# A two-layer token-mixing trunk on one core: hand-set issue order ahead of attention, convolution and pooling sums behind it

## Chip, cores and metric

The kernel runs on one NeuronCore of a Trainium2 chip, in one launch. The metric is the device time of an execution in microseconds (us). The names of the engines in the profile are PE (TensorE, matmuls; PEld its weight loads), DVE (VectorE), ACT (ScalarE), POOL (GpSimd) and SP (SyncE, which here only issues loads and stores).

## What is computed

A trunk of two layers on 512 tokens of 1024 channels, in float32. Each layer mixes the tokens in three branches that are merged by gates, and then runs a wide feed-forward block:

```python
def layer(x, l):
    h = rms_norm(x, g_mix[l])
    proj = h @ w_in[l]
    u_pool, q_lat, kv_lat, u_lru, gate_logit = split(proj)      # 256, 384, 256 + 32, 256, 3 * 1024 columns
    y_pool = pool_mixer(u_pool) @ w_pool_proj[l]                 # means over the last 2, 4, 8, 16 tokens, minus u
    y_mla = attention(q_lat, kv_lat) @ w_mla_o[l]                # 8 heads, causal, rotary part of 32 columns
    y_lru = rg_lru(u_lru) @ w_lru_proj[l]                        # convolution over 4 tokens, gates, linear recurrence
    gates = sigmoid(gate_logit + b_gate[l])                      # three times 1024 channels
    x = x + (gates[0] * y_pool + gates[1] * y_mla + gates[2] * y_lru) @ w_out[l]
    h = rms_norm(x, g_ffn[l])
    return x + square(relu(h @ w_ff1[l])) @ w_ff2[l]             # 4096 inner channels
```

A final norm follows the second layer.

## The kernel before

Channels lie on the 128 partitions, the 512 tokens along the free axis, so x is eight blocks of 128x512. To keep float32's precision, every operand of a matmul is split into a high and a low part in the matmul's reduced format: ScalarE casts the high part, and VectorE (in places POOL) subtracts it from the source. A product is then three matmuls: high by high, high by low, low by high (`three`, `dense`). The split blocks of x, times the norm's gain, are xhm and xlm.

Weights come from DRAM in chunks of 128x1024, one load each on SP's queue into a ring of three buffers (`raw`); `chunk` splits each into whi and wlo, two buffers each (N_W). A chunk thus can be split only when the matmuls of the chunk two before it have been read out.

In the order of the program a layer has these stages:

1. `mixer`, ahead of attention: in_0 to in_9 are the projections of the input (the compressed keys and values ckv, the rotary key kr, the compressed queries ql, the LRU's input, the pooling's input). The norm's factor, rstd, is applied to their results, so they need not wait for it; it is found from the sum of squares of x (`sumsq`: squares on ScalarE, added on POOL), whose sum over partitions is the matmul totm. totckv and totql are the same for the two latent norms. `lru_in` takes in_6 and in_7 through the convolution into u (one scaling and three multiply-adds on VectorE each); `pool_in` takes in_8 and in_9 through the sums over windows on POOL into pm.
2. Attention, head by head: va are the values, ka and qn, qr make keys and queries, s are the scores in four blocks of queries, p the probabilities (minimum and sum on VectorE, exponential on ScalarE), t their transposes, split into pt0h and pt0l (one pair for all heads), o the output. Head h ends with ob, the sum of o's two halves, split into ot (high part on ScalarE, low part on POOL, line 155 by way of line 458). Ahead of heads 0, 2, 4 and 6 stands a gate in the program.
3. `merge`: 24 gates ga_jb in all (24 matmuls each, a product with rstd on VectorE, a tanh on ScalarE), and, once nine of them are issued (LRU_N), `pool_lru_out`: the LRU's two gates for each of two halves (ra_00 to ra_11, three matmuls each), its recurrence, and the pooling's small product (pa). Then `project` combines the branches (pj) and the output projection follows (wo).
4. The feed-forward block (f).

The text is not issued in that order: a scheduler, which simulates the program, orders each engine's instructions when the program is built, within what the data, the buffers and the pools of memory allow. Engines then run their instructions strictly in that order. A pool of memory that is opened later (`mg`, merge) may take the room of one that is closed (`at`, attention); its first writer waits for the last user of that room. The matmuls accumulate in PSUM: three buffers `acc`, two each for scores and transposes, one for o.

The lines that the change touches most:

```python
            a0, a1 = project(C_CKV, "s"), project(C_CKV + 1, "s")
            norm_x(f"m{l}", rstd, sumsq_x(f"m{l}"))
            if l == 0:
                setup_late()
                setup_vectors()
...
            lru_in(0)
            qlat = latent_norm(zq, V_GQ, QR, "ql")
            lru_in(1)
            pool_in(0)
            pool_in(1)
```

`setup_vectors` makes the LRU's constants from its parameters, in some twenty operations of 128x4 on VectorE.

Of the kernel before, what the change touches and what calls it, by code (L numbers as in the profile page):

```python
# [15 lines left out]
P = 128  # L16
D = 1024
# [27 lines left out]
# order of the weight chunks of a layer, each [128, 1024] with the contraction on partitions  # L45
# [7 lines left out]
# columns of the per-channel vectors of a layer  # L53
# [5 lines left out]
# columns of the constants  # L59
# [5 lines left out]
def trunk(ctx: ExitStack, tc, x_in, wts, vecs, consts, out):  # L65
# [12 lines left out]
    # ---- constants and per-channel vectors  # L78
# [15 lines left out]
    # blocks of x and gates share their buffers: x waits in DRAM while the branches are computed  # L94
# [11 lines left out]
    # ---- helpers  # L106
# [37 lines left out]
    def dense(dst, w, acts, off=0):  # L144
        """dst[m, t] = sum_k w[k, m] * act[k, t]"""
        terms = []
        for k, (h, lo_) in enumerate(acts):
            terms += three(blk(w[0], off + k), blk(w[1], off + k), h, lo_)
        matmuls(dst, terms)

    def split(src, hi, lo, scale=None, eng=nc.vector):
        """hi + lo = src * scale, each float32r"""
        if scale is None:
            nc.scalar.copy(hi, src)
            eng.tensor_tensor(lo, src, f(hi), op=ALU.subtract)
        else:
            nc.scalar.activation(hi, src, AF.Copy, scale=scale)
            nc.vector.scalar_tensor_tensor(lo, src, scale, f(hi), op0=ALU.mult, op1=ALU.subtract)  # L158

    def sumsq(blocks, name):  # L160
        s = tmpp.tile([P, S], F32, tag="ssq", bufs=2, name=f"ssq{name}")
        for i, b in enumerate(blocks):
            if i == 0:
                nc.scalar.activation(s, b, AF.Square)
            else:
                q = tmp(f"sq{name}{i}")
                nc.scalar.activation(q, b, AF.Square)
                nc.gpsimd.tensor_tensor(s, s, q, op=ALU.add)
        return s

    def rsqrt_mean(s, n, dst, name):
# [3 lines left out]
        tot = acc(f"tot{name}", "o", 1)  # L175
        matmuls(tot, [(ones, h), (ones, lo)])
        rsqrt(tot, n, dst, name)
# [9 lines left out]
    def sumsq_x(name):  # L187
        return sumsq(x, name)
# [7 lines left out]
    def gained(l, col, name):  # L196
        res = []
        for k in range(KB):
            h = xsp.tile([P, S], F32R, tag="xh", bufs=KB, name=f"xh{name}{k}")
# [5 lines left out]
    def setup():  # L205
        nc.scalar.dma_start(vec, vecs)
        nc.vector.memset(epst, EPS)
        nc.scalar.copy(warm, epst)
        nc.vector.memset(f(ones), 1.0)
        # the first two chunks come by halves, between the first blocks of x  # L210
        raws = [wpool.tile([P, 1024], F32, tag="raw", bufs=N_RAW, name=f"raw0_{c}") for c in range(2)]
        for k in range(KB):
            nc.sync.dma_start(x[k], x_in[k])
            if k < 4:
                c, cols = k // 2, slice(512 * (k % 2), 512 * (k % 2) + 512)
                nc.sync.dma_start(raws[c][:, cols], wts[0, c, :, cols])
        for c in range(2):
            hi, lo = ready[0, c] = wtiles(0, c)
            for i in range(2):
                cols = slice(512 * i, 512 * i + 512)  # L220
                nc.scalar.copy(hi[:, cols], raws[c][:, cols])
                nc.vector.tensor_tensor(lo[:, cols], raws[c][:, cols], f(hi[:, cols]), op=ALU.subtract)
        nc.sync.dma_start(cst, consts)
# [545 lines left out]
```

## Time and profile before

| | |
|---|---|
| median of 3 runs | 1408.4 us |
| runs | 1408.29, 1408.40, 1409.72 us |
| profiled execution, first to last instruction (span) | 1406.1 us |
| TensorE busy | 1379.1 us (98%) |
| VectorE busy | 773.8 us (55%) |
| ScalarE busy | 559.7 us (40%) |
| POOL busy | 320.7 us (23%) |
| mean granted TensorE clock | 0.998 |

The span is that of one execution, taken by the profiler; the time of a run is measured around the whole execution, and for the profiled one only the span is shown. The median run is 2.3 us longer than that span. Busy times overlap, since the engines run side by side; the share of TensorE is an average over stages, and what a change in one stage is worth has to be read from that stage. Matmul records are longer (0.39 us for 512 columns) than the distance from one to the next, because they are pipelined.

### The profile page before, as it was taken

The numbers are of one execution on the slowest core, as the hardware profiler recorded it, in microseconds if no ns is written. First come the engines' busy times: TensorE is split into PE (matmuls) and PEld (weight loads), VectorE is DVE, ScalarE is ACT, GpSimd is POOL, SyncE is SP. The second block draws the span as 40 slices with busy tenths as digits, with TensorE's granted clock in tenths as the row PEclk, the third lists the DMA queues.
The fourth block names the chain that finished last, engine by engine and source line by source line (L and its number), as shares of the span: only waits on it lengthen the run. The fifth ranks groups of instructions, "written<-read, shape, count | busy, mean of one in ns | idle before, by whom it ended". The sixth has DMA issues, their size and how long they took to land.

```text
span 1406.1 us, 16117 instructions
## 1 busy us (share of the span) xinstructions
PE 1379.1 (98%) x6252; PEld 1142.1 (81%) x6252; DVE 773.8 (55%) x1122; ACT 559.7 (40%) x847; POOL 320.7 (23%) x234
## 2 busy tenths in 40 slices
PE   7999999999999999999999999999999999999997
PEld 5877888888888888888887878888888888888886
DVE  8978774574544234443368887655745433344323
ACT  5457683324332112323244777632333221232322
POOL 3265101132322002211115530111232200022112
PEclk9999999999999999999999999999999999999999
DMA  5321122253332323233332212223423233333231
GB/s 200 100 79 61 57 79 100 91 155 100 94 102 92 104 90 105 90 112 113 121 104 85 72 58 73 90 90 105 150 90 105 91 104 90 105 90 105 91 103 62
DMA packets 42124, 137.38 MB, mean 98 GB/s; under 512 B 4672, under 2 KB 6848, under 8 KB 42048
## 3 DMA queue, kind: packets, MB, share of 16 engines
q1 hardware_dynamic: 41328, 135.76, 30.6%
q8 instruction: 49, 0.80, 0.2%
q10 hardware_dynamic: 720, 0.59, 0.1%
q14 instruction: 27, 0.22, 0.0%
HBM read 132.14 MB, written 4.19 MB: 97 GB/s over the span
## 4 chain that ended last, share of the span: by engine, by line
PE 91%; DVE 6%; issue 1%; ACT 1%; DMA 0%; DVEq 0%; ACTq 0%
PE f L116 50%; PE ga L116 17%; PE wo L116 6%; PE pj L116 6%; PE in L116 5%; PE s L116 2%; PE o L452 1%; DVE wlo L138 1%; PE t L444 1%; DVE q L420 1%; PE qr L116 1%; PE ka L116 1%; PE qn L116 1%; DVE qll L158 1%; DVE p L438 0%
## 5 line engine op out<-in xcount | busy, mean ns | idle before, releaser
L137 ACT CAST whi<-raw 128x1024 fp32r<-128x1024 f32 (+1 forms) x236 | 246.7, 1045 | 687.4 <-issue 381.9
L138 DVE TENSOR_TENSOR wlo<-raw,whi 128x1024 fp32r<-128x1024 f32 (+1 forms) x236 | 307.0, 1301 | 162.3 <-ACT whi L137 162.2
L116 PE MATMUL f<-al,whi 128*128 128x512 f32 (+1 forms) x528 | 202.2, 383 | 0.0
L116 PE MATMUL f<-ah,whi 128*128 128x512 f32 (+1 forms) x528 | 202.0, 383 | 0.0
L116 PE MATMUL f<-ah,wlo 128*128 128x512 f32 (+1 forms) x528 | 202.0, 383 | 0.0
L116 PE MATMUL f<-xhf,whi 128*128 128x512 f32 x512 | 199.2, 389 | 0.0
L116 PE MATMUL f<-xlf,whi 128*128 128x512 f32 x512 | 199.2, 389 | 0.0
L116 PE MATMUL f<-xhf,wlo 128*128 128x512 f32 x512 | 199.2, 389 | 0.0
L622 POOL TENSOR_TENSOR ft<-ft 128x512 f32<-128x512 f32 x64 | 94.4, 1477 | 426.9 <-ACT ah L621 426.9
L116 PE MATMUL ga<-xhm,whi 128*128 128x512 f32 x384 | 151.3, 394 | 2.5 <-ACT q L415 2.5
L116 PE MATMUL ga<-xhm,wlo 128*128 128x512 f32 x384 | 151.2, 394 | 0.0
L116 PE MATMUL ga<-xlm,whi 128*128 128x512 f32 x384 | 150.6, 392 | 0.0
L116 PEld LDWEIGHTS f<-al,whi 128*128 128x128 f32 x528 | 99.2, 188 | 19.5
L116 PEld LDWEIGHTS f<-ah,wlo 128*128 128x128 f32 x528 | 99.2, 188 | 19.4
L116 PEld LDWEIGHTS f<-ah,whi 128*128 128x128 f32 x528 | 99.2, 188 | 19.2
L116 PEld LDWEIGHTS f<-xlf,whi 128*128 128x128 f32 x512 | 96.1, 188 | 20.0
L116 PEld LDWEIGHTS f<-xhf,wlo 128*128 128x128 f32 x512 | 96.1, 188 | 20.0
L116 PEld LDWEIGHTS f<-xhf,whi 128*128 128x128 f32 x512 | 96.1, 188 | 19.9
L618 DVE SCALAR_TENSOR_TENSOR ft<-f,rstdf 128x512 f32<-128x512 f32 x64 | 44.1, 692 | 102.1 <-PE f L116 102.0
L116 PEld LDWEIGHTS ga<-xhm,whi 128*128 128x128 f32 x384 | 72.2, 188 | 17.6 <-ACT q L415 3.0
L116 PEld LDWEIGHTS ga<-xlm,whi 128*128 128x128 f32 x384 | 72.2, 188 | 14.3
L116 PEld LDWEIGHTS ga<-xhm,wlo 128*128 128x128 f32 x384 | 72.2, 188 | 14.3
(366 smaller groups left out, 2119.8 us busy)
## 6 DMA issues: line engine op xcount, KB each, us to landing
raw<-wts SPq DMA_DIRECT2D x232, 512.0 KB, 3.5
x<-x_in SPq DMA_DIRECT2D x8, 256.0 KB, 5.4
xr<-x_in SPq DMA_DIRECT2D x8, 256.0 KB, 2.9
saved<-xr SPq DMA_DIRECT2D x8, 256.0 KB, 2.0
xr<-saved SPq DMA_DIRECT2D x8, 256.0 KB, 3.1
out<-xr SPq DMA_DIRECT2D x12, 128.0 KB, 1.8
raw<-wts SPq DMA_DIRECT2D x4, 320.0 KB, 2.9
raw<-wts SPq DMA_DIRECT2D x4, 256.0 KB, 4.5
```

The source lines that it names most:

```text
L116: ins = nc.tensor.matmul(dst, lhsT=a, rhs=b, start=(start and i == 0), stop=(stop and i == n - 1))
L137: nc.scalar.copy(hi[:, :cols], raw[:, :cols])
L138: nc.vector.tensor_tensor(lo[:, :cols], raw[:, :cols], f(hi[:, :cols]), op=ALU.subtract)
L158: nc.vector.scalar_tensor_tensor(lo, src, scale, f(hi), op0=ALU.mult, op1=ALU.subtract)
L420: eng.tensor_tensor(q[o:o + ROPE], qr[src], table[src], op=ALU.mult)
L444: nc.tensor.transpose(tp[:, j, :], blk(probs[i], j), ident)
L452: nc.tensor.matmul(o[:, q0 * P:], lhsT=v[j][:, h, :, :], rhs=pt[c][:, 3 * j + q0:3 * j + 4, :], start=(j == 0 and c == 0), stop=(j == 3 an ...
L618: nc.vector.scalar_tensor_tensor(t, a, 0.0, rstd, op0=ALU.max, op1=ALU.mult)
L622: nc.gpsimd.tensor_tensor(t, t, t, op=ALU.mult)
```

## The change

It has four parts.

**The start.** TensorE gets ten matmuls on a constant block (N_BUSY) ahead of everything else, into the buffers of the transposes. The halves of the first two chunks are loaded in another order among the blocks of x, and the constants come behind the third chunk. in_0 and in_1 go by blocks of x, in turn. `setup_vectors` moves to the merge, behind the first gate that is issued there.

**Ahead of attention.** In a `manual_schedule` PE, DVE and ACT issue in the order of the text. In layer 0 VectorE adds the squares of x, in both layers those of the latents. The sums totm, totckv and totql stand in the middle of in_3, in_5 and in_7, chunks are split one step ahead (`prefetch`), and kr's weights are split in two halves outside the chunks' buffers. in_6 and in_7 are only scaled into u_0 and u_1, in_8 and in_9 into pm_0 and pm_1.

**Behind attention.** The convolution (`conv`, into new tiles cu in the merge's pool) and the sums over windows (`windows`, in place into pm) stand at the head of the merge.

**The branches' small products.** `pool_lru_out` becomes `lru_out` (at nine gates) and `pool_out` (at eleven, POOL_N), each with its own part of the small chunk, so that chunk comes in two loads.

```diff
+N_BUSY = 10
 LRU_N = 9
+POOL_N = 11
+ORDERED = {mybir.EngineType.PE, mybir.EngineType.DVE, mybir.EngineType.Activation}
...
     def setup():
+        busy = tmp("busy", F32R)
+        nc.vector.memset(f(busy), 1.0)
+        nc.vector.memset(epst, EPS)
+        for i in range(N_BUSY):
+            matmuls(acc(f"busy{i}", "t", 2), [(blk(busy, 0), busy)])
...
+        parts = [(c, slice(512 * i, 512 * i + 512)) for i in range(2) for c in range(2)]
         for k in range(KB):
             nc.sync.dma_start(x[k], x_in[k])
-            if k < 4:
-                c, cols = k // 2, slice(512 * (k % 2), 512 * (k % 2) + 512)
-                nc.sync.dma_start(raws[c][:, cols], wts[0, c, :, cols])
+            if k in (0, 3):
+                for c, cols in parts[:2] if k == 0 else parts[2:]:
+                    nc.sync.dma_start(raws[c][:, cols], wts[0, c, :, cols])
...
+            with tc.manual_schedule(engines=ORDERED):
+                if l == 0:
+                    a0, a1 = (acc(f"in{l}_{C_CKV + i}", "s") for i in range(2))
+                    w = [chunk(l, C_CKV + i) for i in range(2)]
+                    for k in range(KB):
+                        for a, c in zip((a0, a1), w):
+                            matmuls(a, three(blk(c[0], k), blk(c[1], k), *xs[k]), start=k == 0, stop=k == KB - 1)
...
+                if l == 0:
+                    ssq = sumsq_x(f"m{l}", nc.vector)
+                prefetch(C_QL)
+                kra = acc(f"in{l}_{C_KR}")
+                matmuls(kra, [(wkr[k], v) for k in range(KB) for v in xs[k]])
+                tot = total(ssq, f"m{l}")
+                prefetch(C_QL + 1)
+                q0, tot = project(C_QL, mid=tot)
...
+                scaled(project(C_LRU), us[0])
+                prefetch(C_POOL)
+                a, tot = project(C_LRU + 1, mid=tot)
...
+                for b in range(2):
+                    pm.append(tmpp.tile([P, S], F32, tag="ssq", bufs=2, name=f"pm{l}_{b}"))
+                    scaled(project(C_POOL + b), pm[b])
...
+    def conv(l, late, us):
+        res = []
+        for b, z in enumerate(us):
+            u = late.tile([P, S], F32, name=f"cu{l}_{b}")
+            cw = lambda j: vcol(l, V_CW + 2 * j + b)
+            nc.vector.tensor_scalar(u, z, cw(3), vcol(l, V_CB + b), op0=ALU.mult, op1=ALU.add)
+            for j in (2, 1, 0):
+                o = 3 - j
+                nc.vector.scalar_tensor_tensor(u[:, o:], z[:, :S - o], cw(j), u[:, o:], op0=ALU.mult, op1=ALU.add)
+            res.append(u)
+        return res
+
+    def windows(l, late, pm):
...
+        for b, z in enumerate(pm):
+            cur = padded(f"pz{l}_{b}", slice(0, P))
+            nc.scalar.copy(cur[:, 8:], z)
...
+            nc.gpsimd.tensor_tensor(z, win, z, op=ALU.subtract)
...
         res = []
         gates = list(early)
+        us = conv(l, mg, us)
+        windows(l, mg, pm)
         for n in range(3 * KB):
             if n == LRU_N:
-                py, ly = pool_lru_out(l, mix, us, pm)
+                ly = lru_out(l, mix, us)
+            if n == POOL_N:
+                py = pool_out(l, mix, pm)
             if n >= len(early):
                 gates.append(gate(l, rstd, xs, n))
+            if l == 0 and n == len(early):
+                with tc.issue_after(last_gate[0]):
+                    setup_vectors()
```

Three places show what becomes of the order. The first is PE in layer 0 at the last head's output, o_7 (from the split probabilities pt0h, pt0l and the values v); ga_41 is a gate's sum, ra are the LRU's gates from the split convolution lyh, lyl. Before:

```order
L452 MATMUL o_7_1628<-pt0h,v_0_689 128x512
L116 MATMUL ga_41_2034<-xhm_136,whi_33_2037 128x512
L116 MATMUL ga_41_2034<-xlm_137,whi_33_2037 128x512
L116 MATMUL ga_41_2034<-xhm_136,wlo_33_2038 128x512
L452 MATMUL o_7_1628<-pt0l,v_0_689 128x512
L452 MATMUL o_7_1628<-pt0h,v_1_699 128x384
L452 MATMUL o_7_1628<-pt0l,v_1_699 128x384
L452 MATMUL o_7_1628<-pt0h,v_2_709 128x256
L452 MATMUL o_7_1628<-pt0l,v_2_709 128x256
L452 MATMUL o_7_1628<-pt0h,v_3_719 128x256
L452 MATMUL o_7_1628<-pt0l,v_3_719 128x256
L116 MATMUL ga_41_2034<-xhm_140,whi_33_2037 128x512
```

With the change:

```order
L505 MATMUL o_7_1588<-pt0h,v_3_679 128x256
L505 MATMUL o_7_1588<-pt0l,v_3_679 128x256
L119 MATMUL ra_00_1859<-lyh_0_1853,whi_15_1849 128x512
L119 MATMUL ra_01_1864<-lyh_0_1853,whi_15_1849 128x512
L119 MATMUL ra_10_1887<-lyh_1_1881,whi_15_1849 128x512
L119 MATMUL ra_00_1859<-lyl_0_1854,whi_15_1849 128x512
L119 MATMUL ra_00_1859<-lyh_0_1853,wlo_15_1850 128x512
L119 MATMUL ra_01_1864<-lyl_0_1854,whi_15_1849 128x512
L119 MATMUL ra_01_1864<-lyh_0_1853,wlo_15_1850 128x512
L119 MATMUL ra_10_1887<-lyl_1_1882,whi_15_1849 128x512
L119 MATMUL ra_10_1887<-lyh_1_1881,wlo_15_1850 128x512
L119 MATMUL ra_11_1892<-lyh_1_1881,whi_15_1849 128x512
```

Where a gate's matmuls stood between and behind those of o_7, the LRU's twelve now follow them directly; behind the last (three of ra_11) come the 24 of ga_30, the 24 of ga_31, the six of pa, and ga_32.

The second is DVE where the convolution is made (L337 and L340 before, L520 and L523 now). Before, between the scaling of in_6 and in_7 and the norm of the queries:

```order
L277 TENSOR_TENSOR lz_0_470<-in_6_472,rstdm_156 128x512
L138 TENSOR_TENSOR wlo_8_590<-raw_8_587,whi_8_589 128x1024
L337 TENSOR_SCALAR u_0_168<-lz_0_470,vec 128x512
L340 SCALAR_TENSOR_TENSOR u_0_168<-lz_0_470,vec,u_0_168 128x512 x3
L277 TENSOR_TENSOR lz_1_546<-in_7_548,rstdm_156 128x512
L337 TENSOR_SCALAR u_1_169<-lz_1_546,vec 128x512
L138 TENSOR_TENSOR wlo_9_633<-raw_9_630,whi_9_632 128x1024
L340 SCALAR_TENSOR_TENSOR u_1_169<-lz_1_546,vec,u_1_169 128x512
L183 SCALAR_TENSOR_TENSOR ntql_525<-totql_521,ntql_525 128x512
L340 SCALAR_TENSOR_TENSOR u_1_169<-lz_1_546,vec,u_1_169 128x512
L184 TENSOR_SCALAR ntql_525<-ntql_525 128x512
```

With the change, behind the sum of head 7's output:

```order
L510 TENSOR_TENSOR ob_7_1597<-ob_7_1597,o_7_1588 64x512
L520 TENSOR_SCALAR cu_0_1606<-u_0_192,vec 128x512
L520 TENSOR_SCALAR cu_1_1611<-u_1_193,vec 128x512
L523 SCALAR_TENSOR_TENSOR cu_0_1606<-u_0_192,vec,cu_0_1606 128x511
L523 SCALAR_TENSOR_TENSOR cu_1_1611<-u_1_193,vec,cu_1_1611 128x511
L523 SCALAR_TENSOR_TENSOR cu_0_1606<-u_0_192,vec,cu_0_1606 128x510
L523 SCALAR_TENSOR_TENSOR cu_1_1611<-u_1_193,vec,cu_1_1611 128x510
L523 SCALAR_TENSOR_TENSOR cu_0_1606<-u_0_192,vec,cu_0_1606 128x509
L523 SCALAR_TENSOR_TENSOR cu_1_1611<-u_1_193,vec,cu_1_1611 128x509
L158 TENSOR_TENSOR lyl_0_1854<-cu_0_1606,lyh_0_1853 128x512
L158 TENSOR_TENSOR lyl_1_1882<-cu_1_1611,lyh_1_1881 128x512
```

The eight operations on u have gone from among the projections to behind ob_7, and the low parts of their results (lyl) follow at once.

The third is ACT where the LRU's and the pooling's small work is done (pyh is the high part of pm, av and th are factors of the recurrence, whi the high part of a chunk). Before, during heads 6 and 7:

```order
L137 CAST whi_29_1935<-raw_29_1933 128x1024
L157 ACTIVATE pyh_1_1860<-pa_1_1892,vec 128x512
L482 ACT_TABLE_LOAD
L482 ACTIVATE th_0_1841<-th_0_1841 128x512
L478 ACT_TABLE_LOAD
L478 ACTIVATE av_1_1878<-tr_1_1866,nsp_83 128x512
L154 CAST ot_2h<-ob_5_1414 64x512
L154 CAST pt0h<-t_62_1534 128x3x128
L137 CAST whi_30_1969<-raw_30_1967 128x1024
```

With the change, behind the last head:

```order
L157 CAST pyh_0_1983<-pm_0_581 128x512
L577 ACT_TABLE_LOAD
L577 ACTIVATE th_0_1870<-th_0_1870 128x512
L573 ACT_TABLE_LOAD
L573 ACTIVATE av_1_1897<-tr_1_1885,nsp_83 128x512
L574 ACTIVATE th_1_1898<-tr_1_1885,sp_82 128x512
L140 CAST whi_15_1979<-raw_15_1977 128x256
L157 CAST lyh_0_1853<-cu_0_1606 128x512
L575 ACTIVATE tr_1_1885<-av_1_1897 128x512
L288 ACTIVATE g_30_1940<-g_30_1940,hb 128x512
L157 CAST pyh_1_1993<-pm_1_608 128x512
L577 ACT_TABLE_LOAD
```

The root th_1 and then whi_30, the chunk for ga_32, are next. The cast of pm_0 now stands ahead of three table loads and of that chunk, and nothing of attention is left between them.

## Rows read from the trace of the kernel before

**Rows 1.** The page: busy us of each engine (share of the span) xinstructions.

```profile
PE 1379.1 (98%) x6252; PEld 1142.1 (81%) x6252; DVE 773.8 (55%) x1122; ACT 559.7 (40%) x847; POOL 320.7 (23%) x234
```

**Rows 2.** Windows: stretch, length, busy us per engine (instructions), granted clock, DMA share, GB/s.

```profile
0.00:20.00 20.00, 11.50 (x29) 7.62 (x30) 16.01 (x33) 13.62 (x25) 10.65 (x14) 1.00 0.74 265
140.00:211.00 71.00, 71.00 (x362) 60.06 (x361) 53.42 (x118) 54.41 (x102) 8.10 (x6) 1.00 0.22 68
700.00:766.00 66.00, 64.56 (x284) 52.77 (x282) 50.27 (x66) 27.44 (x39) 19.51 (x18) 1.00 0.32 97
1380.00:1406.00 26.00, 16.05 (x116) 14.86 (x114) 10.70 (x20) 6.00 (x11) 6.91 (x7) 0.87 0.24 81
```

**Rows 3.** Timeline, TensorE, layer 0: start, length (us), instruction, [idle before <-releaser].

```profile
5.41 0.80 PE L116 MATMUL in<-xhm,whi 128*128 128x512 f32 x1 [5.41 <-ACT whi L221]
...
10.59 0.80 PE L116 MATMUL in<-xlm,whi 128*128 128x512 f32 x1 [1.82 <-DVE xlm L158]
...
16.40 0.59 PE L116 MATMUL in<-xhm,wlo 128*128 128x512 f32 x1
16.83 0.39 PE L116 MATMUL in<-xhm,whi 128*128 128x512 f32 x1
17.06 0.39 PE L116 MATMUL in<-xlm,whi 128*128 128x512 f32 x1
...
24.43 0.39 PE L116 MATMUL totm<-nhm,ones 128*128 128x512 f32 x1
...
75.92 0.39 PE L116 MATMUL ga<-xhm,whi 128*128 128x512 f32 x1
```

**Rows 4.** Timeline, four engines, end of head 7 in layer 0.

```profile
210.75 0.28 PE L452 MATMUL o<-pt0l,v 128*128 128x256 f32 x1
...
211.12 0.58 ACT L456 COPY ob<-o 64x512 f32<-64x512 f32 x1 [2.61 <-PE o L452]
...
211.74 0.69 DVE L457 TENSOR_TENSOR ob<-ob,o 64x512 f32<-64x512 f32 x1 [2.58 <-ACT ob L456]
...
212.46 0.62 ACT L154 CAST ot_3h<-ob 64x512 fp32r<-64x512 f32 x1 [0.76 <-DVE ob L457]
...
213.16 1.29 POOL L155 TENSOR_TENSOR ot_3l<-ob,ot_3h 64x512 fp32r<-64x512 f32 x1 [8.53 <-ACT ot_3h L154]
```

**Rows 5.** Timeline, VectorE: convolution, and a scaled split beside POOL's window additions.

```profile
58.59 0.55 DVE L337 TENSOR_SCALAR u<-lz,vec 128x512 f32<-128x512 f32 x1
...
60.19 0.74 DVE L340 SCALAR_TENSOR_TENSOR u<-lz,vec,u 128x512 f32<-128x512 f32 x1
...
67.25 4.43 DVE L158 SCALAR_TENSOR_TENSOR qll<-zql,vec,qlh 128x512 fp32r<-128x512 f32 x3
```

**Rows 6.** Timeline, POOL: the pooling windows of layer 0, first and last.

```profile
64.47 3.75 POOL L353 TENSOR_TENSOR win<-pz 64x512 f32<-64x512 f32 x1 [1.12 <-DVE pz L277]
...
78.10 3.28 POOL L361 TENSOR_TENSOR win<-win 64x512 f32<-64x512 f32 x2
...
83.44 1.36 POOL L366 TENSOR_TENSOR pm<-win,pz 128x512 f32<-128x512 f32 x1
```

**Rows 7.** Lines, ScalarE 160 to 216 and VectorE 160 to 214: busy, mean ns | idle.

```profile
L137 ACT CAST whi<-raw 128x1024 fp32r<-128x1024 f32 (+1 forms) x8 | 8.2, 1020 | 2.1 <-issue 1.2 <-PE ga L116 0.5 <-ACT p L435 0.4
...
L261 ACT ACTIVATE g<-g,hb 128x512 f32<-128x512 f32 x8 | 5.8, 719 | 0.2
...
L482 ACT ACT_TABLE_LOAD x2 | 2.6, 1283 | 0.0
...
L478 ACT ACTIVATE av<-tr,nsp 128x512 f32<-128x512 f32 x2 | 1.6, 822 | 0.0
...
L138 DVE TENSOR_TENSOR wlo<-raw,whi 128x1024 fp32r<-128x1024 f32 (+1 forms) x8 | 9.7, 1218 | 1.7 <-ACT whi L137 1.7
```

**Rows 8.** Windows behind the kernel's last matmul, columns as in rows 2.

```profile
1397.00:1399.00 2.00, 0.07 (x1) 0.00 (x0) 0.81 (x3) 0.89 (x2) 0.00 (x0) 1.00 0.63 212
1399.00:1401.00 2.00, 0.00 (x0) 0.00 (x0) 1.97 (x4) 0.00 (x0) 1.58 (x2) 0.55 0.14 50
```

More of the change, by code (lines that the diff above doesn't have):

```diff
@@ L269, in mixer, with project, prefetch @@
             at = st.enter_context(tc.tile_pool(name=f"at{l}", bufs=1))
-            def project(c, tag="acc"):
+            def project(c, tag="acc", mid=None):
                 a = acc(f"in{l}_{c}", tag)
-                dense(a, chunk(l, c), xs)
-                return a
+                w = chunk(l, c)
+                terms = [t for k in range(KB) for t in three(blk(w[0], k), blk(w[1], k), *xs[k])]
+                if mid is None:
+                    matmuls(a, terms)
+                    return a
+                matmuls(a, terms[:12], stop=False)
+                res = mid()
+                matmuls(a, terms[12:], start=False)
+                return a, res
+            def prefetch(c):
+                ready[l, c] = chunk(l, c)
             def scaled(a, dst):
@@ L282, in latent_in, with square, add_square @@
                 return z
-            def latent_norm(zs, gcol, width, tag):
-                n = len(zs)
-                r = tmp(f"r{tag}{l}")
-                rsqrt_mean(sumsq(zs, f"{tag}{l}"), width, r, f"{tag}{l}")
+            def square(z, tag, b):
+                q = tmpp.tile([P, S], F32, tag="ssq", bufs=2, name=f"ssq{tag}{l}") if b == 0 else tmp(f"sq{tag}{l}_{b}")
+                nc.scalar.activation(q, z, AF.Square)
+                return q
+            def add_square(s, q):
+                nc.vector.tensor_tensor(s, s, q, op=ALU.add)
@@ L288, in latent_norm, with latent_out @@
+            def latent_out(zs, r, gcol, tag):
                 res = []
-                for b in range(n):
+                for z in zs:
+                    nc.vector.tensor_tensor(z, z, r, op=ALU.mult)
+                for b, z in enumerate(zs):
                     h = mix.tile([P, S], F32R, tag="lat", bufs=10, name=f"{tag}h{l}_{b}")
                     lo = mix.tile([P, S], F32R, tag="lat", bufs=10, name=f"{tag}l{l}_{b}")
-                    nc.vector.tensor_tensor(zs[b], zs[b], r, op=ALU.mult)
-                    split(zs[b], h, lo, vcol(l, gcol + b))
+                    split(z, h, lo, vcol(l, gcol + b))
@@ L308, in mixer @@
-            nc.scalar.copy(wkr[:, :, 0, :], part[:, :, 0, :])
-            nc.vector.tensor_tensor(wkr[:, :, 1, :], part[:, :, 1, :], f(wkr[:, :, 0, :]), op=ALU.subtract)
-            kra = acc(f"in{l}_{C_KR}")
-            matmuls(kra, [(wkr[:, 2 * k:2 * k + 2, :, :], v) for k in range(KB) for v in xs[k]])
-            kr = tmp(f"kr{l}")
-            scaled(kra, kr)
-            zq = [latent_in(project(C_QL), "ql", 0)]
-            ckv = latent_norm(zc, V_GKV, KVR, "ckv")
-            for r, table in ((slice(0, 64), cos), (slice(64, 128), sin)):
-                nc.vector.tensor_tensor(kr[r], kr[r], table[r], op=ALU.mult)
@@ L464, in pool_lru_out, with lru_out @@
+    def lru_out(l, mix, us):
+        w = chunk(l, C_SMALL, 512)
+        res = []
         for b in range(2):
-            py, ly = (tuple(mix.tile([P, S], F32R, tag="lat", bufs=10, name=f"{n}{c}{l}_{b}") for c in "hl") for n in ("py", "ly"))
-            res[0].append(py)
-            res[1].append(ly)
+            ly = tuple(mix.tile([P, S], F32R, tag="lat", bufs=10, name=f"ly{c}{l}_{b}") for c in "hl")
+            res.append(ly)
             u = us[b]
@@ L486, in pool_lru_out, with pool_out @@
             split(u, *ly)
+        return res
+    def pool_out(l, mix, pm):
+        w = chunk(l, C_SMALL, 256, 512)
+        res = []
+        for b in range(2):
+            py = tuple(mix.tile([P, S], F32R, tag="lat", bufs=10, name=f"py{c}{l}_{b}") for c in "hl")
+            res.append(py)
             split(pm[b], *py)
             a = acc(f"pa{l}_{b}")
-            dense(a, w, [py], 4 + b)
+            dense(a, w, [py], b)
             split(a, *py, vcol(l, V_PSC + b))
@@ L585, in trunk @@
     saved = [x_in[k] for k in range(KB)]
-    setup()
     for l in range(L):
-        xs = gained(l, V_GMIX, f"m{l}")
+        if l == 0:
+            with tc.manual_schedule():
+                pieces = setup()
+                xs = gained(l, V_GMIX, f"m{l}", pieces)
+        else:
+            xs = gained(l, V_GMIX, f"m{l}")
         rstd = rstd_tile(f"m{l}")
```

198 lines of the change are left out of this document (112 added, 86 removed).

## Prediction

> **What bounds the kernel now.** I read the page first. TensorE is busy 1379.1 of 1406.1 us [rows 1]: only 27.0 us of the span are not matmul work, and VectorE, the next, is busy for 55% of it. Next come the windows by stage. TensorE is idle for 8.50 us of the first 20, for 1.44 in the stretch of layer 1 ahead of attention, for 9.95 behind the last blocks, and not at all from 140 to 211, which is the second half of layer 0's attention [rows 2]. So whatever the change does there can only add idle time, and its gains must come from the few microseconds at the front. The sum of matmul work hardly changes (ten extra matmuls at the start, ahead of the data). The time therefore moves by TensorE's idle time and by the matmuls that run at the slower clock.
>
> Then the timeline of TensorE. The first matmul starts at 5.41. Until 16.83 the matmuls stand 0.43 us apart, from then on 0.23 (16.83 to 17.06); the first spacing is that of 1.2 GHz, the second that of 2.4 [rows 3]. The column of the clock says 1.00 there [rows 2], so for the start the spacing is what to read. At 10.59 TensorE had stood still 1.82 us for a low part of x that VectorE made late. The sum's first matmul (totm), which follows the 48 matmuls of in_0 and in_1, is at 24.43, the first gate (ga_00) at 75.92 [rows 3].
>
> **The sum** is made against the profiled execution: its span of 1406.1 us and about 2.3 us around it, if it is the median run of 1408.4. The measurement tells about 0.2% (2.8 us) from no change.
>
> **1. Front of layer 0: less.** 264 matmuls stand ahead of ga_00; at 0.227 us they are 59.9 us, so 16.0 of the 75.92 are lost: 5.41 ahead of the first, 8.1 between it and 24.43 (48 matmuls are 10.9), 2.5 behind. Moving the small vector operations away from the start, adding the squares on VectorE, and interleaving in_0 and in_1 by blocks of x go at the 8.1; the ten dummy matmuls go at its slow part, some 19 matmuls at 0.43 instead of 0.23, 3.8 us. The blocks of x and the halves of the first two chunks still come on one queue, so x4 to x7 arrive no earlier, and x1 now stands behind one more half chunk. I let a quarter of the 8.1 stay (2.0) and half of the 2.5: **gain 7.3 us**. Its ends are 2 (clock and loads stay as they are) and 10.6 (everything but the 5.41). The prefetched chunks, the halves of wkr and the sums placed inside in_3, in_5 and in_7 belong to this figure. The moved vector operations cost nothing in their new place: 20-odd of 0.16 us while VectorE is busy 53.4 of 71 us [rows 2].
>
> **2. Front of layer 1: less.** There are 1.44 us of idle time [rows 2]; **gain 1.4**, between 0 and 1.4.
>
> **3. Heads 6 and 7: more, in both layers.** Until now the gates' sums and the LRU's and pooling's small matmuls were TensorE's other work in attention. They needed only u and pm, which were ready before attention. Now both are made behind it; ra_00 and, in order behind it, ga_30 cannot start before. In the new order the gates ga_11 to ga_22 lie among heads 2 to 5, and from the end of ga_22 to o_7 TensorE has 63 small instructions of heads 5 to 7 and nothing else. VectorE has 33 from the gate's product to head 7's sum. At the means of the window 140 to 211 (53.42 us over 118; 71.00 over 362 [rows 2]) that is 14.9 us of VectorE against 12.3 of TensorE. The difference, 2.6, is the lower end. The upper is 8: softmax, transposes, splits and output take turns, and with one pair of split buffers (pt0h, pt0l) for all heads, head 7's splits wait for o_6. I take **5.5 a layer**, about the middle, for the two engines take turns at every block but not all the time.
>
> **4. From o_7 to the LRU's gates: more.** Rows exist for every link. Behind o_7's last matmul (210.75 + 0.28) come the copy, the sum, the high part and, on POOL, the low part, which ends at 214.45: 3.4 us [rows 4]. Today nobody waits, for ga_41 goes on behind it and TensorE has no idle time there [rows 2]. In the change the convolution's first operation waits for just this low part: its tiles take the room that attention's tiles leave. Seven of the eight operations must end before the high part of u_0 can be made: two at 0.55 and five at 0.74, less 0.08 of overlap each [rows 5], 4.3. The cast is 0.62. So ra_00 starts at 3.4 + 4.3 + 0.6 = **8.3 us after o_7**, with TensorE empty. The upper end is 12.0: beside POOL's window additions three such operations took 4.43, 1.48 each instead of 0.74 [rows 5], and the windows now start at the same moment.
>
> **5. From there to ga_32: more.** POOL's chain of both windows took from 64.47 to 84.80, 20.3 us [rows 6]. In the new order four operations follow pm_0: the second of the pair at 78.10 and all behind it, from 79.74 on, 5.1 us. So pm_0 ends 15.2 after the first addition begins, or 12.8 if that long one (3.75) shrinks to the size of the last (1.36). With part 4's 3.4 and the copy ahead (0.6) that is 16.8 to 19.2 after o_7. ScalarE's queue then holds, from pyh_0 to whi_30 in fixed order, three casts at 0.62 (as the high part's [rows 4]), an exponential and a tanh at 0.82, a gate's tanh, two roots and a square, all taken at the tanh's 0.72, a quarter chunk (0.35, an estimate: a third of a whole one), three table loads at 1.28 and the cast of a chunk, 1.02 [rows 7]. They sum to 11.6 us, 10.4 with 0.09 of overlap for each of 13, and wlo_30 adds 1.22 [rows 7]. ga_32 so starts 28.4 to 30.8 after o_7, middle 29.6. (The small chunk, raw_15, now comes in two loads, one more a layer on the load queue; the DMA engines are busy 0.22 of the time from 140 to 211 [rows 2], so I cost it at nothing.) Ahead of it stand 66 matmuls (12 ra, 48 of ga_30 and ga_31, 6 pa), 15.0 us: 13.4 to 15.8 are lost, **14.6**, part 4's wait included.
>
> **6. The clock: more.** After the last matmul of the kernel the granted clock is 1.00 from 1397 to 1399 and 0.55, which is all but 1.2 GHz, from 1399 to 1401 [rows 8]: there it fell behind an engine that stood still. TensorE stands still in part 4 too, and for longer than those 2 us. I let ra and the first gate start at 0.43 us for as long as at the start of the kernel, 11.4 us. That is 26 matmuls; the other 34 take 7.7, so ga_31 ends at 8.3 + 11.1 + 7.7 = 27.1, and since whi_30 needs the buffer that ga_31 reads, ga_32 follows 2.3 later, at 29.4; with part 4's upper end at 33.1. Middle 31.2 instead of 29.6: **1.6 more**, and 0 if the level holds.
>
> The Trainium skill ("TensorE: Matmul & The Clock Gate", HAM oscillation) says that a wait between groups of matmuls makes the next group start slow, each time anew. By that rule the wait ahead of ga_32 would cost once more, which is rival B.
>
> A layer loses 5.5 + 14.6 + 1.6 = 21.7, both 43.4; less 7.3 and 1.4 it is 34.7 more: 1406.1 + 34.7 + 2.3 = **1443 us**. Behind ga_32 the gates follow as before, and no idle time is there to win it back.
>
> **Rivals.**
> **A. The tail is short (25%).** The clock holds, VectorE keeps its speed beside POOL, and parts 3 to 5 stand at their lower ends: 2.6 + 13.4 = 16.0 a layer, 32.0 - 8.7 = 23.3 more, 1432. For it: only one row shows the slow operations. Against it: the row of the clock.
> **B. The slow level comes back ahead of ga_32 (20%).** The gap there, 2.3 us with 6 matmuls in it, is followed by another 26 matmuls at 0.43 instead of 0.23: 5.2 a layer, 1453. Against it: the stop of 1.82 at 10.59 did not keep the clock from rising at 16.83 [rows 3].
> **C. The front gives nothing (3%).** Loads and clock stay as they are, gain 1 instead of 8.7: 1451.
> **D. Faster (4%).** The front gives everything: 27.0 less 9.95 and 5.41 is 11.6, and 3.8 of slow matmuls, 15.4. Heads 6 and 7 keep TensorE full, pm is in time, and the convolution does not wait for head 7's tail, so that of part 4's 8.3 the sum and both splits (0.69, 0.62, 1.29) fall away: 5.7 a layer, 11.4 - 15.4 = -4.0, 1404. It decides from 6.3 a layer down. Against it: the room is attention's own.
> **E. A wash (3%).** The same with the full 8.3: 16.6 - 15.4, 1409 to 1410.
>
> **Numbers.** The forecast has 45% (1435 to 1450), A 25, B 20, C 3, D 4, E 3. So faster 0.04, same 0.03, slower 0.93. The range reaches down to 1423 (A with 3.3 more from layer 0's front, and next to nothing of part 3, 5.2) and up to 1464 (B, part 3 at 8 a layer, the front at 2).
>
> **What would show it.** Right: TensorE idle some 5 us around heads 6 and 7, then a hole of 8 to 12 us between o_7 and ra_00 that ends on the cast lyh; ra and ga_30 0.43 apart; another wait ahead of ga_32 on wlo_30; ga_00 near 69. Wrong: gates between o_7 and ra, or a full TensorE from 190 to 230; then parts 3 to 6 fall together, and with them the sign.

## Result and the profile after the change

The changed kernel takes **1462.88 us** (median; 1462.44 to 1463.28) against 1408.36 (1408.29 to 1409.72): a ratio of 1.0384 [1.0370, 1.0399], 54.5 us slower. The forecast was 1443 with a range of 1423 to 1464: sign and range held, but the loss is over half as large again as the 34.7 us of the sum. The profiled execution's span is 1461.4 us, 55.3 more than before.

The page of the kernel after, engines' busy time and the row of the granted clock in 40 slices; the first line answers to [rows 1]:

```profile
PE 1402.8 (96%) x6262; PEld 1153.4 (79%) x6262; DVE 780.5 (53%) x1136; ACT 564.5 (39%) x855; POOL 300.8 (21%) x221
...
PEclk9999879999999999999999997899999999999999
```

TensorE is now idle for 58.6 us of the span instead of 27.0, and it is busy for 23.7 us more, though only ten matmuls (about 4 us) were added. So a little over half of the loss (31.6 us) is idle time, and most of the rest is matmuls that run slower. The clock's row dips twice, at the end of each layer's attention. The windows of the kernel after in layer 0, columns as in [rows 2]; the first two answer to rows there, the others are the stretches of one tail:

```profile
0.00:20.00 20.00, 17.87 (x66) 12.73 (x67) 13.86 (x25) 14.86 (x25) 0.19 (x4) 1.00 0.86 316
140.00:211.00 71.00, 54.68 (x249) 43.97 (x248) 51.63 (x119) 41.17 (x83) 28.40 (x26) 0.81 0.10 32
...
165.98:173.41 7.43, 5.73 (x34) 4.39 (x33) 7.14 (x22) 6.45 (x17) 0.72 (x1) 1.00 0.22 71
173.41:185.67 12.26, 9.20 (x30) 6.58 (x30) 5.72 (x13) 4.62 (x10) 2.53 (x2) 0.57 0.00 0
185.67:197.23 11.56, 0.01 (x1) 0.00 (x0) 8.81 (x10) 2.95 (x6) 8.89 (x12) 0.50 0.00 1
197.23:202.63 5.40, 5.40 (x13) 3.92 (x14) 2.70 (x3) 3.13 (x5) 5.16 (x5) 0.51 0.00 0
202.63:215.49 12.86, 12.70 (x55) 9.87 (x53) 9.40 (x11) 12.08 (x18) 8.91 (x6) 1.00 0.24 83
215.49:223.14 7.65, 4.18 (x10) 3.07 (x11) 5.90 (x7) 6.08 (x8) 0.00 (x0) 0.78 0.25 69
```

In the first 20 us TensorE is idle for 2.13 instead of 8.50 (some 4 us of its work there are the ten useless matmuls). From 165.98 (the end of ga_22) to 173.41 TensorE waits for 1.70 us in small pieces at the full clock; from there to 185.67, the end of o_7, for 3.06 more, and the mean granted clock is 0.57, so most of that stretch runs at the lower level, 1.2 GHz: **the clock falls inside heads 6 and 7**, not only behind them. Then comes the hole of 11.56, 5.40 us of slow matmuls, the gates, and a second gap with another fall of the clock. Layer 1 has the same picture (the two waits of TensorE that stand first in the kernel's list cover both layers; columns: releaser, us in total, times, longest):

```profile
PE ra L119 <- ACT lyh L157: 23.1, 2, 11.6
PE ga L119 <- ACT lyh L157: 6.1, 2, 3.1
```

The timeline of TensorE after, answering to [rows 3] and, at the tail, to the first of [rows 4]:

```profile
69.22 0.39 PE L119 MATMUL ga<-xhm,whi 128*128 128x512 f32 x1
...
185.26 0.41 PE L505 MATMUL o<-pt0l,v 128*128 128x256 f32 x1
197.23 1.65 PE L119 MATMUL ra<-lyh,whi 128*128 128x512 f32 x3 [11.56 <-ACT lyh L157]
...
202.63 0.40 PE L119 MATMUL ga<-xhm,whi 128*128 128x512 f32 x1
...
218.62 0.47 PE L119 MATMUL ga<-xhm,whi 128*128 128x512 f32 x1 [3.14 <-ACT lyh L157]
...
220.26 0.63 PE L119 MATMUL ga<-xhm,whi 128*128 128x512 f32 x1
220.68 0.63 PE L119 MATMUL ga<-xlm,whi 128*128 128x512 f32 x1
...
222.82 0.49 PE L119 MATMUL ga<-xhm,whi 128*128 128x512 f32 x1
```

ga_00 comes 6.7 us earlier than before (75.92, [rows 3]). ra_00 starts 11.56 behind o_7, ga_32 32.95 behind it (218.62 - 185.67). Behind the hole the matmuls stand 0.43 apart up to 202.63, behind the gap (220.26 to 220.68) again up to 222.82. The other engines between o_7 and ga_32, answering to [rows 4 to 6]:

```profile
187.80 1.26 POOL L158 TENSOR_TENSOR ot_3l<-ob,ot_3h 64x512 fp32r<-64x512 f32 x1 [5.32 <-ACT ot_3h L157]
...
189.09 1.00 DVE L520 TENSOR_SCALAR cu<-u,vec 128x512 f32<-128x512 f32 x2 [2.02 <-POOL ot_3l L158]
...
190.01 7.18 DVE L523 SCALAR_TENSOR_TENSOR cu<-u,vec,cu 128x511 f32<-128x511 f32 x6
...
196.56 1.28 ACT L157 CAST lyh<-cu 128x512 fp32r<-128x512 f32 x2 [6.34 <-DVE cu L523]
...
203.19 1.30 POOL L555 TENSOR_TENSOR pm<-win,pm 128x512 f32<-128x512 f32 x1
...
205.41 0.61 ACT L157 CAST pyh<-pm 128x512 fp32r<-128x512 f32 x1
...
215.82 1.03 ACT L140 CAST whi<-raw 128x1024 fp32r<-128x1024 f32 x1
...
217.81 0.67 DVE L287 TENSOR_TENSOR g<-ga,rstdm 128x512 f32<-128x512 f32 x1
...
218.39 1.21 DVE L141 TENSOR_TENSOR wlo<-raw,whi 128x1024 fp32r<-128x1024 f32 x1
```

The chain of part 4 stands there link by link: the low part ends at 189.06, the convolution starts at 189.09, the high part of the first half follows at 196.56. Its six multiply-adds take 7.18 us beside POOL's windows, 1.20 each where one took 0.74 before [rows 5].

**The account of the span.** Against the kernel before, first instructions of the same tiles: ga_00 -6.7; the first pj of layer 0 at 242.70 instead of 219.05, so 23.7 later, and this tail costs 30.4; the front of layer 1 -1.7 (the last va is 23.3 behind instead of the 25.0 at the feed-forward block); layer 1's tail 30.8. That leaves 2 x 1.3 for a thing that was in no forecast: the output projection wo. Sum: -6.7 - 1.7 + 30.4 + 30.8 + 2.6 = 55.4. The lines of the kernel after on TensorE, 335.2 to 378 (columns as in [rows 7]), show two of wo's three forms:

```profile
L119 PE MATMUL wo<-mgh,whi 128*128 128x512 f32 x62 | 24.3, 392 | 0.0
L119 PE MATMUL wo<-mgh,wlo 128*128 128x512 f32 x61 | 24.3, 398 | 0.0
```

They take 392 to 398 ns each, in the kernel before all 389. Two rows of its timeline, six steps apart:

```profile
335.65 0.40 PE L119 MATMUL wo<-mgh,wlo 128*128 128x512 f32 x1
...
337.06 0.40 PE L119 MATMUL wo<-mgh,wlo 128*128 128x512 f32 x1
```

The six steps take 1.41 us, 0.235 each; over all of wo the mean is 0.233 (44.58 us from its first matmul to its last), before 0.227 (43.29).

### The profile page after: what moved, and what is told of

Same layout as the page of the kernel before. It is cut to its first block, busy times and chain, and to the rows that moved or that the text cites. A ratio compares the mean times of both kernels' runs of the same rounds, so it can differ in the third digit from the quotient of the medians.

```text
span 1461.4 us, 16150 instructions
## 1 busy us (share of the span) xinstructions
PE 1402.8 (96%) x6262; PEld 1153.4 (79%) x6262; DVE 780.5 (53%) x1136; ACT 564.5 (39%) x855; POOL 300.8 (21%) x221
## 4 chain that ended last, share of the span: by engine, by line
PE 87%; DVE 7%; ACT 3%; issue 2%; DMA 1%; POOL 0%; DVEq 0%; ACTq 0%; POOLq 0%
PE f L119 48%; PE ga L119 15%; PE wo L119 6%; PE in L119 6%; PE pj L119 6%; PE s L119 1%; PE o L505 1%; DVE wlo L141 1%; DVE cu L523 1%; DVE q L473 1%; DVE p L491 1%; PE va L119 1%; PE t L497 1%; DVE p L485 1%; PE qr L119 1%
## 5 line engine op out<-in xcount | busy, mean ns | idle before, releaser
L119 PEld LDWEIGHTS f<-xlf,whi 128*128 128x128 f32 x512 | 96.1, 188 | 20.1
L119 PEld LDWEIGHTS f<-xhf,whi 128*128 128x128 f32 x512 | 96.1, 188 | 19.9
```

The lines of the kernel that those rows point to most:

```text
L119: ins = nc.tensor.matmul(dst, lhsT=a, rhs=b, start=(start and i == 0), stop=(stop and i == n - 1))
```

## Experiments

Each run stands against the kernel before (1408.6 us in these); ratios with their 95% intervals. The change is 1462.9.

### Which moved stage costs the time

**e1: both sums back ahead of attention**, as in the kernel before, in its padded tiles; the new front and the two products at nine and eleven gates stay.

```diff
-        us = conv(l, mg, us)
-        windows(l, mg, pm)
...
+            for b in range(2):                  # in mixer, ahead of wv = chunk(l, C_V)
+                z, u = lz[b], us[b]
+                nc.vector.tensor_scalar(u, z[:, 8:8 + S], cw(3), vcol(l, V_CB + b), op0=ALU.mult, op1=ALU.add)
...
```

**e2** has only the convolution ahead, **e3** only the windows.

> Convolution and window sums back ahead of attention, all else as changed. Theory (the tail of attention has no gates to run because the LRU's gates, and every gate behind them, wait for work that waits for attention's room): the tail's cost of some 30 us a layer and the slower output projection vanish, the front's gain of 6.7 and 1.7 stays, so about 1400 us (1398 to 1403). Rival (the cost comes from the other parts: the order set by hand, the small product in two parts, the late small vector operations): it stays above 1420.

> Only the convolution back ahead of attention, the window sums stay behind it. Theory: ra, ga_30 and ga_31 fill heads 6 and 7, but the small pooling product pa stands ahead of ga_32 on TensorE and waits for pm_0, some 17 us of POOL behind o_7, so the hole only moves: 1445 to 1458. Rival (the convolution is the cost): about 1405.

> Only the window sums back ahead of attention, the convolution stays behind it; TensorE's order is that of the changed kernel. Theory: the hole from o_7 to ra_00 shrinks from 11.6 to about 8.3, since the convolution no longer runs beside POOL; ga_32 still hangs on ScalarE's chain, so some 3 us a layer come back, and 1.3 a layer in the output projection if its tiles' addresses are what made it slow: 1452 to 1459. Rival (POOL's sums are what holds the tail): 1435 or less.

Measured: e1 1414.70, 1.0042 [1.0027, 1.0057]; e2 1469.04, 1.0428 [1.0413, 1.0444]; e3 1451.15, 1.0300 [1.0283, 1.0317]. So the two moves together are worth 48.2 of the 54.5 us, but they do not add: taking back the convolution alone makes it 6.2 slower still, taking back the windows alone 11.7 faster. Both missed what was expected: e2 is 11 us above the upper end of its theory, e3 0.9 below the lower end. In e2 the pooled product stands in the LRU's place and waits for POOL's whole chain, which the waits of TensorE show as the first line:

```profile
PE pa L119 <- ACT pyh L157: 36.7, 4, 15.8
```

e3 shows the price of the contention by itself. VectorE's timeline there, with POOL empty:

```profile
189.96 4.04 DVE L549 SCALAR_TENSOR_TENSOR cu<-u,vec,cu 128x511 f32<-128x511 f32 x6
```

And the hole's end on TensorE in e3:

```profile
194.10 1.65 PE L119 MATMUL ra<-lyh,whi 128*128 128x512 f32 x3 [8.48 <-ACT lyh L157]
```

The same six operations take 4.04 instead of 7.18, and the hole is 8.48 instead of 11.56. So 3.1 of the 3.3 us by which the hole was longer than forecast (8.3) come from POOL's windows beside the convolution. e1 missed its expectation: it keeps the early ga_00 (70.22), yet the first pj comes 2.6 us later than before. The longest single wait of TensorE in e1, from its list:

```profile
PE o L541 <- ACT pt0h L157: 1.8, 1, 1.8
```

ScalarE's timeline in e1 shows what stands ahead of that cast:

```profile
188.27 1.28 ACT L613 ACT_TABLE_LOAD   x1
...
190.10 1.03 ACT L140 CAST whi<-raw 128x1024 fp32r<-128x1024 f32 x1
191.15 1.28 ACT L288 ACT_TABLE_LOAD   x1
...
193.07 0.57 ACT L157 CAST pt0h<-t 128x512 fp32r<-128x512 f32 x1
```

The split of the transposes stands behind a table load for the recurrence's root (L613), a gate's chunk, and the table load for a gate's tanh (L288). That named the next suspect, the split of the branches' products.

**e8: as e1, and one product again**: `pool_lru_out` of the kernel before at nine gates, one load of the small chunk.

```diff
-                ly = lru_out(l, mix, us)
-            if n == POOL_N:
-                py = pool_out(l, mix, pm)
+                py, ly = pool_lru_out(l, mix, us, pm)
```

> Convolution and window sums ahead of attention, and the LRU's and the pooling's small products together again, from one load of the small chunk, as they were before the change; the new front stays. Theory (the 8 us that the version with both sums early lost inside attention come from the split small product: a quarter chunk more in the two buffers, pooling's product behind the gates): 1400 to 1405. Rival (attention's own chain on VectorE and ScalarE gives back what the front gains): 1408 or more.

Measured: 1404.08, 0.9973 [0.9962, 0.9984], as expected, 10.6 less than e1 and 0.3% faster than the kernel before. TensorE is busy for all of 170 to 220. So the account is: both sums behind attention 48.2, two products instead of one 10.6 (with the sums ahead), and the new front gives about 4.3 net.

### What the lost time is made of

**e4: more gates ahead of the products** (LRU_N 12, POOL_N 14), so that heads 6 and 7 have gates among them again.

> Three more gates ahead of the LRU (12 instead of 9, pooling's product at 14). Theory: ga_30 to ga_32 fill heads 6 and 7, the loss of 9.7 us a layer there falls to about 1 and the clock stays up through o_7; the hole behind o_7 stays: 1440 to 1449. Rival (heads 6 and 7 are held by their own chain of softmax and splits, whatever fills them): 1455 or more.

Measured: 1448.27, 1.0280 [1.0265, 1.0296], as expected: 7.3 us a layer back. The windows of e4:

```profile
160.00:180.00 20.00, 20.00 (x104) 17.05 (x103) 13.13 (x38) 11.31 (x26) 2.56 (x2) 1.00 0.22 66
```

Where the change stood idle and slow, TensorE is full and at the full clock. Whether the short waits or the small matmuls let the clock fall there (26 of the 63 from ga_22 to the end of o_7 are transposes of 128 columns) is not separated, since the gates fill the waits and stand among the small matmuls at once. The hole stays as it was (11.6): its chain hangs on head 7 and not on the gates.

**e5: thirty useless matmuls behind o_7**, to hold the clock through the hole.

```diff
+        h = xs[0][0]
+        with tc.issue_after(end.ins):            # end: head 7's last matmul
+            for i in range(30):
+                matmuls(acc(f"hole{l}_{i}", "t", 2), [(blk(h, 0), h)])
```

**e6: fourteen useless matmuls behind pa**, in the gap ahead of ga_32.

> The changed kernel with 30 matmuls of no use behind o_7 in each layer, in the hole where TensorE waits for the convolution. Theory: the clock is up again when ra starts, so ra and what follows run 0.23 us apart instead of 0.43, but ga_32 hangs on ScalarE's chain behind POOL's pm_0, so at most 1.5 us a layer come back: 1459 to 1463. Rival (the clock's fall in the hole is what makes the tail so long): 5 us a layer come back, 1453 or less. If the added matmuls are still running when the cast of the convolution is done, up to 1.5 us a layer are lost instead.

> The changed kernel with 14 matmuls of no use between the pooling's product and ga_32 in each layer, where TensorE waits some 3.5 us for a chunk's low part. Theory: the clock falls in that wait and ga_32's first 12 or so matmuls stand 0.43 us apart; filled, they stand 0.23 apart and 2.4 us a layer come back: 1457 to 1459. Rival (the slow matmuls there have another cause than the pause): 1462 to 1464.

Measured: e5 1456.35, 1.0337 [1.0323, 1.0351], between its theories (3.3 us a layer back); e6 1458.25, 1.0352 [1.0338, 1.0366], as expected (2.3 a layer). e5's TensorE:

```profile
184.47 8.82 PE L119 MATMUL hole<-xhm 128*128 128x512 f32 x30
196.25 1.65 PE L119 MATMUL ra<-lyh,whi 128*128 128x512 f32 x3 [2.97 <-ACT lyh L157]
...
199.16 0.63 PE L119 MATMUL ra<-lyh,wlo 128*128 128x512 f32 x1
199.59 0.63 PE L119 MATMUL ra<-lyl,whi 128*128 128x512 f32 x1
...
215.01 0.49 PE L119 MATMUL pa<-pyh,whi 128*128 128x512 f32 x1 [1.09 <-ACT pyh L157]
...
218.22 0.40 PE L119 MATMUL ga<-xlm,whi 128*128 128x512 f32 x1
218.45 0.40 PE L119 MATMUL ga<-xhm,wlo 128*128 128x512 f32 x1
```

The filling ran out 2.97 us too early, and the LRU's gates start slow all the same (in layer 1 too, behind 3.13 us). What it won behind o_7, 2.6 us in layer 0, lies at ga_32: it comes 20.3 us behind ra_00 instead of 21.4, the pieces of waiting ahead of it are short (1.09 is the longest), and the gates behind it stand 0.23 apart. In e6, where no such gap is left, they do too:

```profile
219.13 0.40 PE L119 MATMUL ga<-xlm,whi 128*128 128x512 f32 x1
219.37 0.39 PE L119 MATMUL ga<-xhm,wlo 128*128 128x512 f32 x1
```

So ga_32's slow start is the clock's. In the traces it is worth 1.6 us a layer: from ga_32 to the first pj the change takes 24.1 us, e6 22.5. The rest of e6's 2.3, and a part of e5's 3.3, lies ahead of o_7, where neither edit touches anything. From the last matmul of ga_22 to the end of o_7 the same 63 matmuls in the same order take 19.9 us in layer 0 of the change, 18.5 in e5, 18.9 in e6 and 19.2 in e7, with a mean granted clock from 165 to 186 of 0.74, 0.92, 0.86 and 0.85. So the fall in heads 6 and 7 costs another amount in one trace than in the next, and a difference of 1 us a layer between these runs shows nothing by itself. How much a hole without any stop would give is not measured.

### The spacing of wo

**e7: window tiles 8 columns longer** (528 instead of 520 of float32), so that all tiles behind them begin at a multiple of 64 bytes. **e12: the window tiles in a pool of their own**, opened behind mgh and mgl.

```diff
+                lt = st2.enter_context(tc.tile_pool(name=f"lt{l}", bufs=1))
...
-        windows(l, mg, pm)
+        windows(l, lt, pm)
```

> The changed kernel with the padded tiles of the window sums 528 columns long instead of 520, which moves the tiles behind them in memory (the merged blocks mgh and mgl) by 3 times 32 bytes. Theory: the output projection's matmuls stand 0.2333 apart since the change, and 0.2267 before, because mgh and mgl begin 32 bytes off a multiple of 64; with 528 columns they are back at 0.2267, 1.3 us a layer, 1460. Rival (something else beside them slows the stream): 1462 to 1464 and a spacing of 0.2333.

> The changed kernel, with the tiles of the window sums in memory behind the merged blocks mgh and mgl instead of ahead of them; nothing else. Theory: the output projection's spacing of 0.2333 hangs on where mgh and mgl lie: 0.2267 again, 2.6 us in both layers, 1460. Rival (it hangs on something else of the change): 1462 to 1464 and 0.2333.

Measured: e7 1461.82, 1.0378 [1.0364, 1.0392], no difference, wo still at 394 ns a record; the first idea fell. e12 1458.85, 1.0357 [1.0342, 1.0371], 4.0 less than the change, of which 2.6 are wo's (43.29 us a layer again); for the other 1.4 no cause was looked for. One of its lines of wo, the other forms are the same:

```profile
L119 PE MATMUL wo<-mgh,whi 128*128 128x512 f32 x64 | 24.9, 389 | 0.0
```

The instructions of wo are the same, so the spacing hangs on where tiles lie in memory; the window tiles, put ahead of mgh and mgl, had moved these. The runs above agree: e2, which keeps the window tiles there, has 0.233, and e1, e3 and e8, which do not, have 0.227. The traces show no addresses, so which property decides stays open.

### The front, and a version that beats both

**e11: as e8, without the ten useless matmuls** at the start (N_BUSY 0).

> As e8, without the ten matmuls of no use at the start. Theory: the clock then comes up later, some 15 of in_0's and in_1's matmuls more stand 0.43 apart, 3 us: 1406 to 1408. Rival (the start waits for data, not for the clock): 1403.5 to 1405.

Measured: 1403.59, 0.9964 [0.9950, 0.9978]: no slower than e8. TensorE's timeline at the start of e11, whose matmuls stand 0.43 apart until 9.18:

```profile
9.18 0.48 PE L119 MATMUL in<-xhm,whi 128*128 128x512 f32 x1
9.50 0.40 PE L119 MATMUL in<-xlm,whi 128*128 128x512 f32 x1
```

And of e8:

```profile
6.32 0.40 PE L119 MATMUL in<-xhm,wlo 128*128 128x512 f32 x1
6.55 0.39 PE L119 MATMUL in<-xhm,whi 128*128 128x512 f32 x1
```

In e8 the full speed is there at 6.32, in e11 at 9.50 (two of the ten matmuls stand only behind in_0's first two). By totm the lead has shrunk to 0.3 us (24.65 and 24.98), for e8 then waits for x: 0.23 us for a high part and 0.28 for a low one, 0.19 in all in e11. By ga_00 it is the other way round (70.32 and 69.32). TensorE reaches kra 0.3 us earlier in e8, at 39.3, but waits there for 1.6 us, in e11 for 0.2: kra's buffer in PSUM comes free behind the norms' small operations on ScalarE and VectorE, and they are 1.0 us later in e8, where ScalarE's table load stands behind its wait for totm (25.34) and in e11 ahead of it (22.86). So e11 has this second difference besides the ten matmuls; what these alone bring is 0.3 us at totm, and none of it was left at ga_00.

**e9: the convolution inside attention.** As e8, but it reads u unpadded, writes one new tile and u_0's room, and is held until the gate ga_10 is issued, ahead of head 7 in the text; for the room, the two blocks of ones in memory become one. **e10** holds it only until ga_02.

```diff
+                if h == 7:
+                    with tc.issue_after(last_gate[0]):
+                        cu = [mix.tile([P, S], F32, name=f"cu{l}_0"), us[0]]
...
```

> As e8 (sums ahead of attention, one small product), but the convolution is held back until the gate ga_10 is formed, so that its eight operations lie spread over heads 3 and 4 and no longer ahead of the values' splits; for the room the two blocks of ones in memory become one. Theory: TensorE's waits of 0.85 us a layer for the values' splits and of 0.86 for the first queries go, and nothing is late behind it: 1400 to 1403. Rival (VectorE is as full there, and the softmax is late instead): 1405 or more.

> As e9, but held only until ga_02 is formed (heads 1 and 2, where VectorE is fullest). Theory: between e8 and e9, 1402 to 1405. Rival: slower than e8 (over 1405), since softmax is what TensorE waits for there.

Measured: e9 **1401.62**, 0.9951 [0.9938, 0.9963], the fastest of all (0.5% under the kernel before); e10 1406.37, 0.9983 [0.9975, 0.9992], 2.3 slower than e8, its rival's case. In e9 the waits for the values' splits and for the first queries are gone, as expected. The first windows of attention in e10 (columns as in [rows 2]):

```profile
80.00:110.00 30.00, 27.97 (x137) 22.78 (x136) 28.55 (x51) 19.86 (x40) 15.16 (x11) 1.00 0.24 75
110.00:140.00 30.00, 27.33 (x138) 22.13 (x137) 29.24 (x74) 21.12 (x50) 14.16 (x10) 1.00 0.20 63
```

The same in e9:

```profile
80.00:110.00 30.00, 28.80 (x144) 24.06 (x145) 27.80 (x53) 19.93 (x43) 15.84 (x12) 1.00 0.23 71
110.00:140.00 30.00, 28.42 (x145) 23.60 (x144) 28.67 (x69) 21.54 (x50) 12.42 (x9) 1.00 0.17 57
```

The eight operations run from 100.9 to 119.2 in e10 and from 120.3 to 139.1 in e9. VectorE is nearly full in both stretches of both, and TensorE has 4.70 us of idle time in e10 against 2.78 in e9; over both layers it waits 5.9 us for the softmax and the splits of its results on VectorE (stat, pt0l, pt1l) in e10 and 3.1 in e9. So the earlier place makes the softmax later; that VectorE has more room in the later one is read from these rows and was not tested further.

## Why the prediction was right in sign and too small in size

**Parts 1 and 2 held.** Forecast gains of 7.3 and 1.4 against 6.7 and 1.7. But the reason given for half of part 1 fell: the ten matmuls do raise the clock earlier, and of that 0.3 us were left at totm, where TensorE had waited for x, and nothing at ga_00 (e8 against e11).

**Part 3 had the waiting right and no clock in it.** It put 5.5 us a layer on heads 6 and 7 taking turns. The idle time there is 1.70 + 3.06 = 4.8. The whole loss is 10.1, by difference: the tail's 30.4 less 18.0 between o_7 and ga_32 (32.95 less the 15.0 of work) and 2.3 behind it. The other 5.3 are for the most part matmuls at the slow level: the 30 in the window 173.41 to 185.67 (0.57) were busy for 9.20 us, which at the spacings of the full clock would be 4.1. This term was mis-sized by 4.6 a layer: part 6 let the clock fall only behind o_7, where TensorE is empty, and not in the stretch of short waits ahead of it.

**Part 4 had the chain right and took the wrong end of its range.** Forecast 8.3, measured 11.56; the upper end of 12.0 had been priced with just the contention that e3 shows. The row for it was there [rows 5], and the sum used the undisturbed one, though the same paragraph says that the windows start at the same moment.

**Parts 5 and 6** forecast ga_32 31.2 us behind o_7; it came at 32.95, 1.7 more. Up to the end of ga_31 two errors nearly cancelled (27.8 us behind o_7 against part 6's 27.1): the hole was 3.3 longer, and the matmuls behind it ran slow for 5.40 us, not for the forecast 11.1. From there ga_32 took 5.1 us, not 2.3, and by another chain than the text has. pm_0 was ready at 204.49, but its cast stands at 205.41 with no idle time of ScalarE before it: what held was ScalarE's own queue, which starts on the LRU's gates. e3, where pm is made ahead of attention, agrees: ga_32 still stands 20.5 us behind ra_00, against 21.4. whi_30 did not wait for the buffer that ga_31 reads (read out at 213.7) but for its turn on ScalarE (215.82), and was ready at 216.85. What ends just ahead of ga_32 (218.62) is VectorE's product of ga_31 with rstd (217.81 to 218.48), which empties the PSUM buffer that ga_32 takes (pa's two sums hold the others), and which stands behind the recurrence; the profile names lyh, whose cast ends 0.07 later and which ga_32 does not read. The 0.34 us for wlo_30 come only behind ga_32's second matmul. So the middle of part 5 was nearly right, and its links pm_0 and the chunk's buffer were not what bound.

**Rival B happened at under half its price.** Behind the gap of 3.14 us the gates ran slow until 222.82. From ga_32 to the first pj that is 2.3 us a layer above the full spacing, 1.6 of it the clock's (e6), instead of 5.2. The Trainium skill ("TensorE: Matmul & The Clock Gate", HAM oscillation) says that a wait between groups of matmuls, if it is long enough, makes the next group start slow, each time anew. The traces agree behind the waits of 3.14 and (e5) 2.97 us, and not behind e5's 1.09.

**Missed altogether:** wo, 1.3 a layer. Nothing in the diff touches its instructions; the new tiles only moved its operands.

Per layer these are 4.6 + 1.7 + 2.3 + 1.3 = 9.9, in both 19.8; the front of layer 0 gives 0.6 less than forecast and that of layer 1 0.3 more, together 20.1. The distance from 34.7 is 19.8 to the 54.5 of the runs and 20.6 to the span's 55.3. A, C, D and E are out. The time stands at the range's upper edge, and that it stands inside is in part luck: the upper end was built from a front of 2 and a B of 5.2 a layer, which did not come, while the clock in heads 6 and 7 and wo, which no bound held, came in their place.

## What to carry to other kernels

Work that an engine does beside another stage costs nothing only while the other engines' queues have room there. Moved behind that stage, it costs its whole chain, and the stage that lost its filler costs again, here in waits (4.8 us a layer) and in matmuls at the slower clock (about 5); so price short waits and slow matmuls together. When two parts of a chain move to one place, take the durations of the disturbed row, not of the lone one; and when tiles are added to a pool, compare the spacing of matmuls that the diff does not touch.

## What the hardware showed that was not expected

- Matmuls of one form with the same instructions (wo) stand 0.227 us apart in the kernel before and 0.233 in the change, and e12 brings them back by the order of the pools alone.
- TensorE's granted clock fell inside attention's last heads, where TensorE was at work for most of the time (5.73 of 7.43 us) and, in layer 0, had no wait longer than 0.91 us ahead of the fall.
- Six multiply-adds of VectorE take 4.04 us with POOL empty (e3) and 7.18 beside its additions. The Trainium skill ("SBUF — State Buffer", Who interferes with whom) holds that a VectorE operation with two inputs in SBUF (the on-chip memory of the tiles) and a POOL operation that reads SBUF contend, and that the second to issue is shut out until the first has ended. At strict turns, an estimate, each would wait for one of POOL's additions (1.4 us in the change), some 2 us each. The rows show 1.20 each, a stretching by 1.8, less than that.
- Useless matmuls raise the clock at the start and buy 0.3 us at totm and nothing at ga_00 (e8 against e11); in a gap they buy what the slow start behind it costs (e6), if they reach to its end, which in e5 they did not.
